# Inputs laid out by the launch: x turned, the columns of w_ada over the partitions, weights as blocks

## The chip, the core and the metric

The kernel runs on one core of a Trainium2 chip. The metric is device time in microseconds (us); the time before is the median of three runs, 811.69 us (811.64 to 811.93). An execution has been profiled with the hardware profiler, and all rows below come from it. Names: PE is TensorE (matrix products), PEld its weight loads, DVE is VectorE, ACT is ScalarE, POOL is GpSimd, SP is SyncE, which issues most of the DMAs. The laying out of the inputs, which the change adds, is done by the host ahead of the launch and is not in the measured time.

## What is computed

One decoder layer for 256 tokens of width 2048 with float32 weights: a conditioned norm, one wide projection, two attention mixers, two branch projections and an output projection.

```python
ada = c @ w_ada + b_ada                       # c: (1, 2048), w_ada: (2048, 6144)
shift, scale, gate = jnp.split(ada, 3, axis=-1)
h = rms_norm(x, g_pre) * (1.0 + scale[:, None, :]) + shift[:, None, :]
proj = h @ w_in                               # (256, 2048) @ (2048, 11824)
...                                           # sparse attention (A), dilated windows (B)
merged = jax.nn.sigmoid(ma) * ya + jax.nn.sigmoid(mb) * yb
out = merged @ w_out
return x + (gate[:, None, :] * rms_norm(out, g_post))
```

## The kernel before

**Split products.** A product takes h, or its like, as a high and a low part (xH, xL), and each weight tile as a high part (wH, rounded by ACT, L539) and a low part (wL, the remainder by DVE, L540). Three matmuls add up: wH with xH (L609), wH with xL (L611), wL with xH (L614); lines L599 to L604 are the same with the sides exchanged. Only the first pass, over the first 128 of the 2048 features, multiplies unsplit f32 (L585, L589).

**The stream of items.** All weights come as a list of items of up to 128 x 1024 floats, in a fixed order: `w` items are weight tiles, `ada` items are pieces of w_ada for shift and scale, `gate` items are the rest of w_ada, `ck` items belong to attention A. SP loads them (`dma`, L512 to L521) into seven buffers named raw; when an item's buffer is free again the seventh item after it is issued. Three items ahead of the product, `prep` splits a weight (L539, L540) or adds an `ada` item to a sum (L556, L558: sum += raw times one value of c per partition). `main` issues the products and `evac` empties the PSUM banks.

**Features in passes.** h is not known at once, since scale and shift need 16 MB of w_ada. So features come in groups (feature blocks of 128: 0; 1 to 2; 3 to 6; 7 to 9; 10 to 12; 13 to 15). For each group the `ada` items run ahead of the weight items that need it. When its last item is in, `make_h` (L273) turns the sums on PE (L282: the 128 partial sums of a column lie over the partitions, so a transpose brings them into a row), adds them on DVE (L283), adds the bias and forms h from xT, the normed and turned x.

**The start.** x arrives in two megabytes with tokens on partitions. ACT and DVE each square half (L170, L172, with a sum along the row), DVE forms 1/rms (L180 to L192). c, b_ada and g_pre arrive as rows and are turned on PE (L143). For feature block 0 the sums over w_ada are PE products (L241) and a DVE share (L257, L259). `keep_warm` issues products whose result nobody reads. The first h ends with L299 (tile hF), and L589 is the first product of the stream.

**The side work.** `side_main` is a list of steps, of which one is issued beside each item: x of each later group is normed on POOL (L223) and turned on PE (L230), then the tables of angles, masks, and the two attentions. Position weights pe_ck and pe_cv are turned there, too (L808). Within each engine the order is what the tile scheduler makes of this program; `behind` adds an order without a wait.

Of the kernel before, what the change touches and what calls it, by code (L numbers as in the profile page):

```python
# [44 lines left out]
def hybrid_block(tc, x, c, positions, w_ada, b_ada, g_pre, g_post, w_in, pe_ck, pe_cv, w_ck1, w_ck2,  # L45
                 w_cv1, w_cv2, w_br_a, w_br_b, w_out, out):
    with ExitStack() as ctx:
        _build(ctx, tc, x, c, positions, w_ada, b_ada, g_pre, g_post, w_in, pe_ck, pe_cv, w_ck1, w_ck2,
               w_cv1, w_cv2, w_br_a, w_br_b, w_out, out)


def _build(ctx, tc, x, c, positions, w_ada, b_ada, g_pre, g_post, w_in, pe_ck, pe_cv, w_ck1, w_ck2,
           w_cv1, w_cv2, w_br_a, w_br_b, w_out, out):
# [36 lines left out]
    vc = work.tile([16, 128], F32, name="vc", tag="PT", bufs=2)  # L90
    vec = work.tile([48, 128], F32, name="vec", tag="PT", bufs=2)
    xs = big.tile([128, NT, D], F32, name="xs", tag="ma")
    for t in range(NT):
        DMA.dma_start(xs[:, t, :], x[0, t * 128:(t + 1) * 128, :])
    A.dma_start(vc, c[0].rearrange("(a p) -> a p", p=128))
    A.dma_start(vec[0:32, :], b_ada[0, 0:2 * D].rearrange("(a p) -> a p", p=128))
    A.dma_start(vec[32:48, :], g_pre[0].rearrange("(a p) -> a p", p=128))
# [27 lines left out]
    cT, bT, gT = vecT[:, 0:16], vecT[:, 16:48].rearrange("p (h k) -> p h k", h=2), vecT[:, 48:64]
# [26 lines left out]


    n0 = (PASSES[0][1] - PASSES[0][0]) * 128
    nb0 = n0 // 128
    ST = big.tile([128, 4, 1024], F32, name="ST", tag="mb")
    acc0 = ST[:, 1, 0:2 * n0].rearrange("p (h n) -> p h n", h=2)
    raws0 = []
    for q in range(4):
        r = wp.tile([128, 4, 2, n0], F32, name="raw0", tag="raw", bufs=RAW)  # L160
        for half in range(2):
            DMA.dma_start(r[:, :, half], rows(w_ada[0], 4 * q, 4, half * D, n0))
        raws0.append(r)


    ssq = const.tile([128, NT], F32)
    ssp = const.tile([128, NT, 2], F32)
    for t in range(NT):
        lo, hi = slice(0, D // 2), slice(D // 2, D)
        i_sq = A.activation(ST[:, 2], xs[:, t, lo], AF.Square, accum_out=ssp[:, t, 0:1])  # L170
        with behind(i_id, i_c):
# [1144 lines left out]
```

## Time and profile before

| What | Value |
|---|---|
| Median of three runs | 811.69 us |
| Span of the profiled execution, first to last instruction | 808.8 us |
| PE busy | 790.9 us, 98% |
| DVE busy | 673.6 us, 83% |
| ACT busy | 443.2 us, 55% |
| POOL busy | 90.1 us, 11% |
| Read from memory | 190.38 MB |
| First product of the stream (L589) | 18.18 us after the span's start |

The page gives a single time for the profiled execution, its span. A record of a matmul lasts until its result has drained, so records overlap, and a busy PE isn't PE at its peak; the distance from one record's start to the next says what a matmul costs in a stream. A chain of waits follows the end back: at each step to what released it. A table by stage cuts the span into stretches.

### The profile page before, as it was taken

The numbers are of one execution on the slowest core, as the hardware profiler recorded it, in microseconds if no ns is written. First come the engines' busy times: TensorE is split into PE (matmuls) and PEld (weight loads), VectorE is DVE, ScalarE is ACT, GpSimd is POOL, SyncE is SP. The second block draws the span as 40 slices with busy tenths as digits, with TensorE's granted clock in tenths as the row PEclk, the third lists the DMA queues.
The fourth block names the chain that finished last, engine by engine and source line by source line (L and its number), as shares of the span: only waits on it lengthen the run. The fifth ranks groups of instructions, "written<-read, shape, count | busy, mean of one in ns | idle before, by whom it ended". The sixth has DMA issues, their size and how long they took to land.

```text
span 808.8 us, 11963 instructions
## 1 busy us (share of the span) xinstructions
PE 790.9 (98%) x4181; PEld 665.5 (82%) x4181; DVE 673.6 (83%) x1033; ACT 443.2 (55%) x731; POOL 90.1 (11%) x111
## 2 busy tenths in 40 slices
PE   7999999999999999999999999999999999999995
PEld 4588988899887889788889999888888888888884
DVE  6799899999996979898878997778796888867464
ACT  2767564443444655587776777555644344444451
POOL 4300000000000027064312121001100000000000
PEclk9999999999999999999999999999999999999998
DMA  9999989999896578644344435557789989976523
GB/s 334 361 371 294 321 295 321 344 309 341 268 365 218 168 223 260 192 143 144 118 145 122 140 111 168 180 178 237 227 267 296 304 287 327 316 246 222 190 102 104
DMA packets 106951, 193.25 MB, mean 239 GB/s; under 512 B 7594, under 2 KB 36618, under 8 KB 106252
## 3 DMA queue, kind: packets, MB, share of 16 engines
q1 hardware_dynamic: 105344, 189.16, 71.2%
q10 hardware_dynamic: 1548, 3.34, 1.2%
q8 instruction: 33, 0.54, 0.3%
q14 instruction: 26, 0.21, 0.1%
HBM read 190.38 MB, written 2.10 MB: 238 GB/s over the span
## 4 chain that ended last, share of the span: by engine, by line
PE 90%; DVE 5%; DMA 2%; issue 1%; ACT 1%; POOL 0%; DVEq 0%; SPq 0%; POOLq 0%; ACTq 0%
PE mm L609 23%; PE mm L611 23%; PE mm L614 22%; PE mm L599 3%; PE mm L604 3%; PE mm L601 3%; PE mm L589 2%; PE pt_ps L999 1%; PE sA L963 1%; DVE wL L540 1%; DMA xs<-in_x_dram 1%; PE mm L585 1%; DVE ST L558 1%; DMA raw<-in_w_in_dram 1%; PE pvb_ps L1140 1%
## 5 line engine op out<-in xcount | busy, mean ns | idle before, releaser
L539 ACT ACTIVATE wH<-raw 128x1024 fp32r<-128x1024 f32 (+2 forms) x268 | 267.9, 1000 | 276.3 <-PE mm L611 204.4
L540 DVE TENSOR_TENSOR wL<-raw,wH 128x1024 fp32r<-128x1024 f32 (+2 forms) x268 | 315.6, 1181 | 90.6 <-ACT wH L539 85.6
L609 PE MATMUL mm<-wH,xH 128*128 128x512 f32 (+2 forms) x616 | 237.3, 387 | 0.0
L611 PE MATMUL mm<-wH,xL 128*128 128x512 f32 (+2 forms) x616 | 234.4, 382 | 0.0
L614 PE MATMUL mm<-wL,xH 128*128 128x512 f32 (+2 forms) x616 | 189.9, 383 | 0.0
L611 PEld LDWEIGHTS mm<-wH,xL 128*128 128x128 f32 x616 | 115.9, 188 | 20.1
L609 PEld LDWEIGHTS mm<-wH,xH 128*128 128x128 f32 x616 | 115.8, 188 | 20.0 <-ACT mm L629 0.3
L614 PEld LDWEIGHTS mm<-wL,xH 128*128 128x128 f32 x616 | 113.6, 188 | 22.0 <-DVE wL L540 0.3
L558 DVE SCALAR_TENSOR_TENSOR ST<-raw,vecT,ST 128x768 f32<-128x768 f32 (+2 forms) x75 | 76.5, 1020 | 1.8 <-DMA raw<-in_w_ada_dram 1.5
L599 PE MATMUL mm<-xH,wH 128*128 128x256 f32 x240 | 62.5, 281 | 0.0
L601 PE MATMUL mm<-xL,wH 128*128 128x256 f32 x240 | 62.0, 279 | 0.0
L609 PE MATMUL mm<-wH,yH 128*128 128x512 f32 x128 | 50.4, 394 | 0.0
L609 PE MATMUL mm<-wH,mH 128*128 128x512 f32 x128 | 50.0, 391 | 0.0
L611 PE MATMUL mm<-wH,yL 128*128 128x512 f32 x128 | 49.9, 389 | 0.0
L611 PE MATMUL mm<-wH,mL 128*128 128x512 f32 x128 | 49.8, 389 | 0.0
L604 PE MATMUL mm<-xH,wL 128*128 128x256 f32 x240 | 49.2, 279 | 0.0
L599 PEld LDWEIGHTS mm<-xH,wH 128*128 128x128 f32 x240 | 45.0, 188 | 0.1
L601 PEld LDWEIGHTS mm<-xL,wH 128*128 128x128 f32 x240 | 45.0, 188 | 0.1
L558 DVE SCALAR_TENSOR_TENSOR gacc<-raw,vecT,gacc 128x1024 f32<-128x1024 f32 x32 | 41.0, 1283 | 0.0
L614 PE MATMUL mm<-wL,mH 128*128 128x512 f32 x128 | 39.8, 389 | 0.0
L614 PE MATMUL mm<-wL,yH 128*128 128x512 f32 x128 | 39.4, 389 | 0.0
L604 PEld LDWEIGHTS mm<-xH,wL 128*128 128x128 f32 x240 | 37.3, 188 | 0.0
(306 smaller groups left out, 1016.3 us busy)
## 6 DMA issues: line engine op xcount, KB each, us to landing
raw<-in_w_in_dram SPq DMA_DIRECT2D x165, 512.0 KB, 4.6
raw<-in_w_ada_dram SPq DMA_DIRECT2D x48, 512.0 KB, 5.0
raw<-in_w_ada_dram SPq DMA_DIRECT2D x48, 384.0 KB, 4.9
raw<-in_w_out_dram SPq DMA_DIRECT2D x32, 512.0 KB, 4.8
raw<-in_w_br_a_dram SPq DMA_DIRECT2D x16, 512.0 KB, 6.4
raw<-in_w_br_b_dram SPq DMA_DIRECT2D x16, 512.0 KB, 5.8
raw<-in_w_in_dram SPq DMA_DIRECT2D x29, 256.0 KB, 3.5
raw<-in_w_ada_dram SPq DMA_DIRECT2D x24, 256.0 KB, 5.6
```

The costliest lines, as they stand in the source:

```text
L539: highest[0] = A.activation(H, raw, AF.Copy)
L540: lowest[0] = V.tensor_tensor(L, raw, H.bitcast(F32), op=OP.subtract)
L558: V.scalar_tensor_tensor(acc, r, cc, acc, op0=OP.mult, op1=OP.add)
L585: T.matmul(job.ps[t][:, b * S:(b + 1) * S], lhsT=it.raw[:, j, c0:c0 + 128], rhs=hj, start=(first and j == 0 and b == 0), stop=(last and j ...
L589: i_mm = T.matmul(job.ps[t][:, :job.n], lhsT=hj[:, t * 128:(t + 1) * 128], rhs=it.raw[:, j, cs], start=(first and j == 0), stop=(last and ...
L599: T.matmul(ps, lhsT=it.H[:, j, bs], rhs=sH[:, it.kt0 + j, :], start=(first and j == 0 and b == 0), stop=False, skip_group_check=True)
L601: T.matmul(ps, lhsT=it.H[:, j, bs], rhs=sL[:, it.kt0 + j, :], start=False, stop=False, skip_group_check=True)
L604: T.matmul(ps, lhsT=it.L[:, j, bs], rhs=sH[:, it.kt0 + j, :], start=False, stop=(last and j == it.nk - 1), skip_group_check=True)
L609: T.matmul(ps, lhsT=sH[:, it.kt0 + j, ts], rhs=it.H[:, j, cs], start=(first and j == 0), stop=False, skip_group_check=t in job.seeded)
L611: T.matmul(ps, lhsT=sL[:, it.kt0 + j, ts], rhs=it.H[:, j, cs], start=False, stop=False, skip_group_check=t in job.seeded)
L614: T.matmul(ps, lhsT=sH[:, it.kt0 + j, ts], rhs=it.L[:, j, cs], start=False, stop=(last and j == it.nk - 1), skip_group_check=t in job.seeded)
L963: T.matmul(o, lhsT=QT[:, u.t, h // 2, h % 2, :], rhs=KTt[:, hl, :, 0:128] if u.t == 0 else KTt[:, hl, u.br, :], start=(hl == 0), stop=(hl ...
```

## The change

The host lays the inputs out anew: x turned (feature on the partition), c, b_ada, g_pre and the position weights already as columns in one array of 128 x 96, positions as one array, and for shift and scale the array w_ss, in which a partition holds one column of w_ada, so 2048 values in a row. All weight items lie one behind the other in the order in which the kernel loads them, each as a block in which a partition's values are one contiguous piece (4 KB for 1024 floats).

In the kernel, c is spread over all partitions once (four f32 products with a row of ones, L142, copied to cB). An `ada` item is then 128 columns by 1024 rows, and DVE multiplies it with cB and sums along the row in one instruction (L529), of which a feature block needs four: 60 in all beyond block 0, where there were 80 instructions over 72 items. The turns of sums and their reductions (L282, L283) go. x is squared without a sum and summed over the partitions with one-column products (L186); 1/rms is spread by two products (L225), POOL multiplies the turned x with it (L751), and the turns of x (L230) go. Weight items, products, passes and attention stay as they are.

```diff
-    for t in range(NT):
-        DMA.dma_start(xs[:, t, :], x[0, t * 128:(t + 1) * 128, :])
...
+    A.dma_start(crow, d_in["c"])
+    for q in range(4):
+        DMA.dma_start(xs[:, 4 * q:4 * q + 4, :], d_in["xT"][:, 4 * q:4 * q + 4, :])
+    A.dma_start(small, d_in["small"])
+    A.dma_start(pos_i, d_in["pos"])
...
+            i_c = T.matmul(ps, lhsT=ones[0:1, :], rhs=crow[:, j * 512:(j + 1) * 512], start=True, stop=True)
...
+    def c_halves():
+        for j in (1, 3):
+            last = A.activation(cB[:, j // 2, 512:1024], c_ps[j], AF.Copy)
+        return last
...
+        if q < 3:
+            with behind(*last_sq):
+                last_sq = [A.activation(sq, xq, AF.Square)]
+            G.tensor_tensor(sq[:, 0:512], sq[:, 0:512], sq[:, 512:1024], op=OP.add)
+            if q == 0:
+                with behind(*last_sq):
+                    last_sq = [c_halves()]
...
+                    i_ss = T.matmul(ss_ps[:, t, 0:1], lhsT=sq[:, k * S + t * 128:k * S + (t + 1) * 128],
+                                    rhs=ones[:, 0:1], start=(q == 0 and k == 0 and t == 0),
...
+    def sum0(q, half, after):
+        r = raws0[q][:, half]
+        with behind(after):
+            return V.scalar_tensor_tensor(r, r, 1.0, cB[:, q // 2, q % 2 * 512:(q % 2 + 1) * 512], op0=OP.mult,
+                                          op1=OP.mult, accum_out=sums0[:, half, q:q + 1])
...
-                for i in range(m):
-                    for j in range(n):
-                        T.transpose(ps[:, i, j, :], acc[:, half + i, j * 128:(j + 1) * 128], ident)
-                V.tensor_reduce(AB[:, half:half + m, a:b], ps, axis=AX.X, op=OP.add)
...
+    def weights(name, kt0, nk, c0, n):
+        at = placed[0]
+        plan.append((name, kt0, nk, c0, n))
+        placed[0] += 128 * nk * n
+        w = d_in["weights"]
+        return bass.AP(tensor=w.tensor, offset=w.offset + at, ap=[[nk * n, 128], [1, nk * n]])
...
+            if it.kind == "ada":
+                r = raw[:, 0, :]
+                V.scalar_tensor_tensor(r, r, 1.0, cB[:, it.q], op0=OP.mult, op1=OP.mult,
+                                       accum_out=sums[:, it.half, it.kt0, it.q:it.q + 1])
...
-            for t in range(NT):
-                with behind(*first_h):
-                    x_norm(G, a, b, t)
-                    x_turn(a, b, t)
-                yield
+            G.tensor_tensor(xT[a], xs[:, a:b, :], rstdB[:, None, :].to_broadcast([128, b - a, S]), op=OP.mult)
+            yield
```

**Order on PE around the first products.** Before, from the turn of b_ada and g_pre to the second pass (ada_ps: sums for block 0, x_ps: turns of x for block 0, xT_ps: turns of later x):

```order
L143 MATMUL v_ps<-ident,vec 128x48
L241 MATMUL ada_ps<-vecT,raw_136 128x128 x8
L251 MATMUL x_ps<-ident,xs 128x128 x2
L241 MATMUL ada_ps<-vecT,raw_142 128x128 x6
L264 MATMUL ada_ps<-ones_r,ST 128x128 x2
L589 MATMUL mm<-raw,hF 128x512 x8
L230 MATMUL xT_ps<-ident,xs 128x128 x2
L589 MATMUL mm<-raw,hF 128x256 x2
L230 MATMUL xT_ps<-ident,xs 128x128 x4
L282 MATMUL ada_ps<-ident,ST 128x128 x4
```

Now, with six, eight and six warm-ups (L135) behind the first, the second and the third row (c_ps: c spread, ss_ps: sums of squares, rB_ps: 1/rms spread):

```order
L142 MATMUL c_ps<-ST,ones_r 128x512 x4
L186 MATMUL ss_ps<-ones_r,sqs 128x1 x20
L225 MATMUL rB_ps<-ident,rstd 128x128 x2
L564 MATMUL mm<-raw,hF 128x512 x8
L564 MATMUL mm<-raw,hF 128x256 x2
L564 MATMUL mm<-raw,hF 128x304 x2
L564 MATMUL mm<-raw,hF 128x512 x12
L560 MATMUL mm<-hF,raw 128x256 x16
L582 MATMUL mm<-wH,xH 128x512
```

Nothing stands between the products of the first pass any more, and ahead of them the sums of w_ada have left PE.

**Order on ACT at the start.** Before (xs: x, v_ps: turned rows, rtx: the root):

```order
L170 ACTIVATE ST,ssp<-xs 128x1024 x2
L145 ACTIVATE vecT<-v_ps 128x48
L186 ACTIVATE rtx<-ssq 128x2
L268 ACTIVATE ST<-x_ps 128x256
L301 ACTIVATE xH<-hF 128x256
```

Now (sqs: squares, ST<-c_ps: the two copies of spread c):

```order
L172 ACTIVATE sqs<-xs 128x1024
L153 ACTIVATE ST<-c_ps 128x512 x2
L172 ACTIVATE sqs<-xs 128x1024 x2
L179 ACTIVATE sqs<-xs 128x512
L212 ACTIVATE rtx<-ssq 128x2
L232 ACTIVATE rstdB<-rB_ps 128x256
L284 ACTIVATE xH<-hF 128x256
```

The second and third square now stand behind the copies of c, which wait for PE.

**Order on DVE at the start, now** (raw_139 to raw_148: block 0 of w_ss, sums_184: its row sums). Before, the two squares with their sums and the five multiplications of block 0 stood here:

```order
L148 COPY ST<-c_ps 128x512 x2
L181 TENSOR_TENSOR sqs<-xs 128x512
L194 SCALAR_TENSOR_TENSOR raw_139,sums_184<-raw_139,ST 128x512 x2
L194 SCALAR_TENSOR_TENSOR raw_142,sums_184<-raw_142,ST 128x512 x2
L205 TENSOR_SCALAR ssq<-ss_ps 128x2
L194 SCALAR_TENSOR_TENSOR raw_145,sums_184<-raw_145,ST 128x512
L218 SCALAR_TENSOR_TENSOR rstd<-tfx,rtx 128x2
L194 SCALAR_TENSOR_TENSOR raw_148,sums_184<-raw_148,ST 128x512 x2
L260 SCALAR_TENSOR_TENSOR ST<-xs,small,rB_ps 128x256
L275 TENSOR_REDUCE AB<-sums_184 128x2
L283 TENSOR_SCALAR hF<-ST,AB 128x256
```

Four of the eight row sums of block 0 stand behind the mean square, three of them behind the root.

More of the change, by code (lines that the diff above doesn't have):

```diff
@@ L155, in _build @@
-    nb0 = n0 // 128
-    ST = big.tile([128, 4, 1024], F32, name="ST", tag="mb")
-    acc0 = ST[:, 1, 0:2 * n0].rearrange("p (h n) -> p h n", h=2)
+    with behind(keep_warm(8)):
+        c_ps = []
+        for j in range(4):
+            ps, _ = product_bank("c_ps")
+            i_c = T.matmul(ps, lhsT=ones[0:1, :], rhs=crow[:, j * 512:(j + 1) * 512], start=True, stop=True)
+            c_ps.append(ps)
+    with behind(i_c):
+        i_warm = keep_warm(6)
+    with behind(i_mask):
+        for j in (0, 2):
+            i_cV = V.tensor_copy(cB[:, j // 2, 0:512], c_ps[j])
@@ new lines, in _build @@
+    sums0 = const.tile([128, 2, 5], F32)
+    def sum0(q, half, after):
[3 more added lines that the diff above has]
+                                          op1=OP.mult, accum_out=sums0[:, half, q:q + 1])
+    with behind(i_sq):
+        V.tensor_copy(sums0[:, 0, 4:5], bT[:, 0, 0:1])
+        i_sum = V.tensor_scalar(sums0[:, 1, 4:5], bT[:, 1, 0:1], 1.0, None, op0=OP.add)
@@ L182, in rsqrt @@
+    for q in range(2):
+        for half in range(2):
+            i_sum = sum0(q, half, i_sum)
+    ssq = const.tile([128, NT], F32)
+    with behind(i_sum):
+        i_ssq = V.tensor_scalar(ssq, ss_ps[:, :, 0], 1.0 / D, EPS, op0=OP.mult, op1=OP.add)
+    i_sum = sum0(2, 0, i_ssq)
     def rsqrt(dst, ms, name):
@@ L191, in rsqrt @@
                                    op0=OP.mult, op1=OP.mult)
-        V.scalar_tensor_tensor(dst, tf, 1.5, rt, op0=OP.add, op1=OP.mult)
-        return ih
+        return V.scalar_tensor_tensor(dst, tf, 1.5, rt, op0=OP.add, op1=OP.mult)
     rstd = const.tile([128, NT], F32)
-    rsqrt(rstd, ssq, "x")
+    with behind(i_sum):
+        i_sum = rsqrt(rstd, ssq, "x")
+    rB_ps = psum.tile([128, S], F32, name="rB_ps", tag="pv")
+    for t in range(NT):
+        i_rB = T.matmul(rB_ps[:, t * 128:(t + 1) * 128], lhsT=rstd[:, t:t + 1].to_broadcast([128, 128]), rhs=ident,
+                        start=True, stop=True)
+    with behind(i_ss):
+        keep_warm(8)
+    with behind(i_rB):
+        keep_warm(6)
+    rstdB = const.tile([128, S], F32)
+    A.activation(rstdB, rB_ps, AF.Copy)
     xH = big.tile([128, KT, S], F32R, name="xH")
@@ L245, in _build @@
-    with behind(turn):
-        ada0_part(0)
-    x0_ps = psum.tile([128, nb0, S], F32, name="x0_ps", tag="pt")
-    for t in range(NT):
-        i_x = x_norm(V, 0, nb0, t)
-        for j in range(nb0):
-            T.transpose(x0_ps[:, j, t * 128:(t + 1) * 128], xs[:, t, j * 128:(j + 1) * 128], ident)
-    on_dve = 5
-    for kt in range(4, 4 + on_dve):
-        r, cc = raws0[kt // 4][:, kt % 4], cT[:, kt:kt + 1]
-        if kt == 4:
-            with behind(i_x):
-                V.tensor_scalar(acc0, r, cc, None, op0=OP.mult)
-        else:
-            V.scalar_tensor_tensor(acc0, r, cc, acc0, op0=OP.mult, op1=OP.add)
@@ L426, in w_item @@
         it.n = sum(j.n for j in jobs)
-        it.src = rows(w, kt0, nk, c0, it.n)
+        it.src = weights(w, kt0, nk, c0, it.n)
         return it
```

284 lines of the change are left out of this document (116 added, 168 removed).

## The prediction

> **What bounds the kernel now.** I read the page's busy table first, then a table by stage (columns: the stretch in us, then length and busy time with instruction counts of PE, PEld, DVE, ACT and POOL, then granted clock, share of the DMA engines, GB/s), then the chain of waits.
>
> ```profile
> PE 790.9 (98%) x4181; PEld 665.5 (82%) x4181; DVE 673.6 (83%) x1033; ACT 443.2 (55%) x731; POOL 90.1 (11%) x111
> ```
> ```profile
> 0.00:18.20 18.20, 13.33 (x75) 8.40 (x75) 12.52 (x38) 4.51 (x10) 7.47 (x14) 1.00 0.94 327
> 18.20:60.00 41.80, 41.80 (x169) 28.24 (x170) 35.52 (x88) 28.95 (x54) 8.84 (x7) 1.00 1.03 367
> 60.00:200.00 140.00, 140.00 (x792) 122.72 (x790) 133.94 (x164) 73.04 (x92) 0.00 (x0) 1.00 0.94 319
> 200.00:243.00 43.00, 43.00 (x195) 35.39 (x193) 41.15 (x48) 19.18 (x20) 0.00 (x0) 1.00 0.92 313
> 300.00:480.00 180.00, 176.00 (x1141) 155.56 (x1140) 160.74 (x307) 125.26 (x294) 57.06 (x71) 1.00 0.51 155
> 480.00:800.00 320.00, 320.00 (x1555) 268.51 (x1554) 239.80 (x311) 160.66 (x220) 10.41 (x9) 1.00 0.70 227
> ```
> ```profile
> PE 90%; DVE 5%; DMA 2%; issue 1%; ACT 1%; POOL 0%; DVEq 0%; SPq 0%; POOLq 0%; ACTq 0%
> ```
>
> From 18.2 us to 800 TensorE stops only in attention (4.0 us idle of 180). So there are three parts: a start in which PE produces nothing, a long stretch in which PE work is time, and a tail that the change leaves alone. Work taken from PE in the middle is worth its full spacing; work taken from DVE, ACT or the DMA queues there is worth nothing unless PE waits for it. DVE runs at 96% from 60 to 243 us and so must not get more work.
>
> **The change part by part.** *The start.* Rows of the timeline (start, length, engine, line, operation, tile, count, idle before and its releaser):
>
> ```profile
> 1.85 3.32 PE L137 MATMUL warm<-identb 128*128 128x512 bf16 x8 [1.85 <-DVE identb L80]
> 5.27 3.20 PE L137 MATMUL warm<-identb 128*128 128x512 bf16 x14
> 6.04 1.06 ACT L170 ACTIVATE ST<-xs 128x1024 f32<-128x1024 f32 x1 [2.42 <-DMA xs<-in_x_dram]
> 8.70 1.23 DVE L172 SCALAR_TENSOR_TENSOR ST<-xs 128x1024 f32<-128x1024 f32 x1 [1.16 <-DMA xs<-in_x_dram]
> 9.86 0.08 DVE L172 DVE_READ_ACCUMULATOR ST<-xs 128x1 f32 x1
> 10.62 0.16 DVE L180 TENSOR_SCALAR ssq<-ssq 128x2 f32<-128x2 f32 x1
> 11.63 0.16 DVE L192 SCALAR_TENSOR_TENSOR rstd<-tfx,rtx 128x2 f32<-128x2 f32 x1
> 12.76 2.40 PE L241 MATMUL ada_ps<-vecT,raw 128*128 128x128 f32 x20
> 17.44 0.69 DVE L299 TENSOR_SCALAR hF<-ST,AB 128x256 f32<-128x256 f32 x1
> 18.18 7.13 PE L589 MATMUL mm<-raw,hF 128*128 128x512 f32 x16 [1.24 <-DVE hF L299]
> 19.35 0.60 ACT L702 ACTIVATE CV<-mm 128x512 f32<-128x512 f32 x1 [0.77 <-PE mm L589]
> 18.61 0.43 DVE L303 TENSOR_TENSOR xL<-hF,xH 128x256 fp32r<-128x256 f32 x1 [0.48 <-ACT xH L301]
> ```
> ```profile
> L994 POOL TENSOR_TENSOR P<-P,cf 128x512 f32<-128x512 f32 x24 | 27.5, 1144 | 83.7 <-DVE cf L992 59.4 <-PE mm L614 10.8 <-ACT mm L629 7.8
> ```
>
> Before, the first product starts at 18.18. For the new start I add these durations along the new order. x's two megabytes landed at 6.04 and 8.70, so the four half-megabyte pieces land near 4.7, 6.0, 7.4 and 8.7. PE is through with eight warm-ups at 5.1. The four products that spread c over the partitions are f32 with 512 columns; such a product is two records of the L589 row, 7.13/16 = 0.45 us each, less its drain 0.43, so 0.87: four end at about 8.75. ACT's order is square 0 (4.7 to 5.8), two copies of c, squares 1 and 2, half a square. The second copy needs c's fourth product: 8.75 + 0.60 = 9.35. Squares 1 and 2 then end at 10.4 and 11.5 although x was there at 6.0 and 7.4; the half ends at 12.1. POOL's additions (512 elements, 1.14) end at 11.6 and 12.7. PE's sums of squares come in this order: four for piece 1 after 11.6, four for piece 2 after 12.7, eight for piece 3. Each is an f32 product, two records; L241 gives 2.40/20 = 0.12 a record, so 0.24: 13.7, then 15.6. From there all is on DVE. Mean square 0.16; a row sum of 512, from 1.23 for 1024 with the read of 0.08, is about 0.69; from L180's end (10.78) to L192's end (11.79) the root takes 1.0; three more row sums 2.07; x0 0.43; the small sum 0.16; hF 0.35 to 0.69. 15.7 + 0.16 + 0.69 + 1.0 + 2.07 + 0.43 + 0.16 + 0.5 = 20.7. **First product at 20.7, +2.5 us.** Low end: if one-column products cost next to nothing and squares never wait, the last weights set it. At x's pace (1 MB in 2.66) the 2 MB of raw0 land at 14.0, then 0.69 + 0.43 + 0.16 + 0.5 gives 15.8, -2.4. High end: POOL's additions and the additions' readers late by 1 us, clock lost (below): +4.5.
>
> *PE work removed.* Thirty transposes of x (L230), thirty of the sums (L282), two of the position weights (L808), in groups of two to four:
>
> ```profile
> L230 PE MATMUL xT_ps<-ident,xs 128*128 128x128 f32 x30 | 4.9, 272 | 0.0
> L282 PE MATMUL ada_ps<-ident,ST 128*128 128x128 f32 x30 | 4.8, 274 | 0.5 <-DVE AB L283 0.5
> 38.22 0.60 PE L282 MATMUL ada_ps<-ident,ST 128*128 128x128 f32 x4
> 38.66 3.62 PE L585 MATMUL mm<-hF,raw 128*128 128x256 f32 x16
> 46.01 0.49 PE L230 MATMUL xT_ps<-ident,xs 128*128 128x128 f32 x3
> 46.26 0.48 PE L609 MATMUL mm<-wH,xH 128*128 128x512 f32 x1
> 242.85 0.40 PE L611 MATMUL mm<-wH,xL 128*128 128x512 f32 x1
> 243.73 0.55 PE L282 MATMUL ada_ps<-ident,ST 128*128 128x128 f32 x3 [0.49 <-DVE AB L283]
> ```
>
> The means are lengths; records overlap. What counts is the distance to the next product: four in 38.66 - 38.22 = 0.44 (0.11 each), three in 46.26 - 46.01 = 0.25 (0.083 each). 24 stand in groups of two and four: 2.6 us; 36 in threes: 3.0. The two L808 are allowed 0.2 each. **-6.0 us**, between -5.0 (every transpose at 0.083, L808 nothing) and -6.6. The stage table shows no PE idle where they stood, so nothing else fills the place. *One stall.* At 242.85 the next product would follow after 0.23; PE waits until 243.73 for L283, which no longer exists: **-0.65**, between 0 and -0.9.
>
> *Shift and scale on DVE.* Here lies the cover that has to hold.
>
> ```profile
> L558 DVE SCALAR_TENSOR_TENSOR ST<-raw,vecT,ST 128x512 f32<-128x512 f32 x15 | 11.8, 789 | 1.2 <-DMA raw<-in_w_ada_dram 1.0
> L558 DVE SCALAR_TENSOR_TENSOR ST<-raw,vecT,ST 128x768 f32<-128x768 f32 x45 | 45.5, 1012 | 0.4 <-DMA raw<-in_w_ada_dram 0.2
> L558 DVE SCALAR_TENSOR_TENSOR ST<-raw,vecT,ST 128x1024 f32<-128x1024 f32 x15 | 19.1, 1275 | 0.3 <-DMA raw<-in_w_ada_dram 0.3
> L172 DVE SCALAR_TENSOR_TENSOR ST<-xs 128x1024 f32<-128x1024 f32 x2 | 2.5, 1226 | 1.6 <-DMA xs<-in_x_dram 1.6
> L283 DVE TENSOR_REDUCE AB<-ada_ps 128x3 f32<-128x384 f32 x6 | 3.3, 550 | 0.0
> L283 DVE TENSOR_REDUCE AB<-ada_ps 128x4 f32<-128x512 f32 x3 | 2.1, 689 | 2.4 <-PE ada_ps L282 2.4
> ```
>
> The rows before cost 11.8 + 45.5 + 19.1 = 76.4 us and 5.4 for the reductions. Sixty row sums have the form of L172, 1.226: 73.6. DVE gets 8.2 us lighter by 243 us and had 6.3 + 6.1 + 1.9 = 14.2 idle: hidden, 0. *DMA layout.* The bytes of every item stay, the pieces grow to a whole row of a partition; PE waits for no landing after 18.2 us: 0. SP is left with 32 issues fewer, none is moved past another. *xT on POOL*: 3840 elements at 1.144/512 are 8.6 us, done by 27, and PE first needs them near 38: 0. Ten ACT copies go from an engine at 55%: 0. *Attention.* Fewer side steps shift which product stands beside which score; its 4.0 us of idle may move either way: 0, within 2 us.
>
> Sum: 2.5 - 6.0 - 0.65 = -4.15. The page gives the profiled execution by its span, 808.8; the median of the runs, 811.69, lies 2.9 above it, taken as what surrounds the span and kept. 808.8 - 4.15 + 2.9 = **807.5 us**.
>
> **The rivals.** *The start is not late* (0.24). The squares' chain ends before DVE is through with its row sums. For it: one-column products may be far cheaper than 0.24. Against it: squares 1 and 2 stand behind c's fourth product whatever these cost. First product at 15.8 to 18.2: 802.6 to 805.
>
> *A cold start* (0.12). PE does only one-column products and waits from 10 to 15.6. The first eight warm-ups took 3.32 us, fourteen later ones 3.20, that is 0.42 and 0.23 each. Eight products' worth at the slow pace cost 3.32 - 8 x 0.23 = 1.5 more: 809.0. Against it: the fourteen warm-ups around the root. [...]
>
> *The transposes' time comes back as waits* (0.08). With PE earlier by 3 us, wL arrives late between 60 and 243 us, where DVE has 8 us of idle; the gain of 6.65 is lost and the start remains: 811.7 to 814.
>
> *Row sums at half speed* (0.04; slower). If a multiply of two f32 tiles with a sum took twice L172's 1.226, sixty would add 73.6 us; 14.2 + 8.2 of room leaves 51 on the path: about 859. It decides from (22.4 + 4.15)/60 = 0.44 us more, 1.67 a sum. [...] The trace speaks against it: L172 is that form, though both its sources are one tile, and is no slower than L558's 1.275.
>
> **How the numbers follow.** Forecast 0.50, then 0.24, 0.12, 0.08, 0.04, and 0.02 for a mishap in attention. 0.2% is 1.6 us, about what a measurement of this kernel can tell from none. Faster (under 810.1): 0.50 + 0.24 + 0.10 = 0.84. Same: 0.02 + 0.08 = 0.10. Slower: 0.06. The range reaches from the early start, 802.8, to the edge of the third rival, 811.0.
>
> **What would show it.** The first L564 record at 19.5 to 22 with ACT idle before square 1; L529 near 1.23 us; no PE idle from there to 300 us; PE's busy time some 6 us less. Wrong if PE waits for wL before 243 us, or if L564 begins before 18.

## The result: slower, not faster

The changed kernel took 817.44 us (median of four executions, 814.65 to 819.82) against 811.66 for the kernel before on the same chip: a ratio of 1.0069, 95% interval 1.0044 to 1.0094. Forecast were 807.5 us and a range up to 811.0. One thing has to be known to read its times: the unaltered kernel has two starts, which differ by 5 us, and an execution has the one or the other (eight of eleven took 814.2 to 816.0, three 818.9 to 819.8). The profile below is of the shorter one, 814.65 us with a span of 812.9, which is 4.1 more than the 808.8 before.

The busy table of the changed kernel, and its table by stage in the stretches of the prediction (stretch, length, busy time and count of PE, PEld, DVE, ACT, POOL, granted clock, DMA share, GB/s):

```profile
PE 795.0 (98%) x4125; PEld 663.7 (82%) x4125; DVE 671.2 (83%) x1074; ACT 441.3 (54%) x722; POOL 90.8 (11%) x109
```
```profile
0.00:18.20 18.20, 16.02 (x63) 9.57 (x64) 11.63 (x31) 6.15 (x8) 5.81 (x12) 0.85 0.89 330
18.20:60.00 41.80, 38.71 (x119) 22.22 (x118) 33.70 (x93) 24.60 (x45) 11.24 (x6) 0.90 0.79 278
60.00:200.00 140.00, 139.25 (x780) 121.52 (x779) 134.11 (x199) 72.87 (x91) 0.00 (x0) 1.00 0.92 333
...
243.00:300.00 57.00, 57.00 (x263) 47.11 (x262) 45.16 (x68) 31.08 (x41) 6.35 (x11) 1.00 0.60 202
300.00:480.00 180.00, 176.59 (x1130) 155.19 (x1129) 156.19 (x301) 123.29 (x287) 55.76 (x70) 1.00 0.49 157
```

All of the loss lies ahead of 80 us. From 18.2 to 60 us, where PE had no idle time before, it now idles 3.1 us, the clock reads 0.90, and the loads move 278 GB/s instead of 367. From 200 to 300 us all is as forecast, PE has no idle time there; the half microsecond that it waited at 243 is gone.

**The start.** Rows of the timeline of the changed kernel (start, length, engine, line), then the table by stage in narrow stretches:

```profile
5.38 3.86 PE L142 MATMUL c_ps<-ST,ones_r 1*128 1x512 f32 x8
9.17 2.74 PE L135 MATMUL warm<-identb 128*128 128x512 bf16 x6
11.70 2.26 PE L186 MATMUL ss_ps<-ones_r,sqs 128*128 128x1 f32 x16
14.29 3.75 PE L186 MATMUL ss_ps<-ones_r,sqs 128*128 128x1 f32 x24 [0.32 <-POOL sqs L173]
17.90 3.15 PE L135 MATMUL warm<-identb 128*128 128x512 bf16 x7
20.84 1.06 PE L225 MATMUL rB_ps<-ident,rstd 128*128 128x128 f32 x4
23.87 12.48 PE L564 MATMUL mm<-raw,hF 128*128 128x512 f32 x32
...
9.77 1.99 ACT L172 ACTIVATE sqs<-xs 128x1024 f32<-128x1024 f32 x2
...
10.90 3.33 POOL L173 TENSOR_TENSOR sqs<-sqs 128x512 f32<-128x512 f32 x2 [3.61 <-ACT sqs L172]
...
10.73 0.69 DVE L194 SCALAR_TENSOR_TENSOR raw<-raw,ST 128x512 f32<-128x512 f32 x1
11.57 1.53 DVE L194 SCALAR_TENSOR_TENSOR raw<-raw,ST 128x512 f32<-128x512 f32 x1
13.04 1.74 DVE L194 SCALAR_TENSOR_TENSOR raw<-raw,ST 128x512 f32<-128x512 f32 x1
```
```profile
9.20:10.50 1.30, 1.30 (x5) 0.47 (x5) 1.23 (x4) 1.23 (x2) 0.00 (x0) 0.50 0.97 312
18.00:20.80 2.80, 2.80 (x8) 1.10 (x7) 2.65 (x13) 0.20 (x1) 0.00 (x0) 0.50 0.66 259
```

The first product comes at 23.87, not at 20.7. Up to ACT's squares all is within 0.6 us of the forecast. Then three things differ. PE runs at half clock from 9.2 to 12.6 and again from 16.0 to 22.8 (it reads 0.50): six warm-ups take 2.74 us, so the sums of squares begin at 11.7, and their later records are 0.21 us apart instead of 0.11. POOL's additions take 1.67 us each instead of the 1.14 of the forecast (the first one, which met no row sum, took 1.26), and DVE's row sums beside them 1.53 and 1.74 instead of 0.69: they hold each other up. And the spreading of 1/rms (L225) stands behind warm-ups of 0.43 us, so that it starts 1.2 us after 1/rms is there.

**Pass 0.** Rows of the timeline, what SP's queue waits for DVE's row sums in the whole execution (us in total, times, longest), and a row of the table by stage:

```profile
22.40 11.09 POOL L751 TENSOR_TENSOR xT<-xs,rstdB 128x512 f32<-128x512 f32 x5 [8.17 <-ACT rstdB L232]
24.30 2.01 DVE L286 TENSOR_TENSOR xL<-hF,xH 128x256 fp32r<-128x256 f32 x1 [0.48 <-ACT xH L284]
26.23 2.83 DVE L529 SCALAR_TENSOR_TENSOR raw<-raw,ST 128x1024 f32<-128x1024 f32 x1
29.09 0.33 SPq L501 DMA_DIRECT2D raw<-in_weights_dram  x1
31.75 2.82 DVE L529 SCALAR_TENSOR_TENSOR raw<-raw,ST 128x1024 f32<-128x1024 f32 x1
34.50 1.21 DVE L529 SCALAR_TENSOR_TENSOR raw<-raw,ST 128x1024 f32<-128x1024 f32 x1
37.17 3.67 PE L564 MATMUL mm<-raw,hF 128*128 128x512 f32 x8 [0.82 <-DMA raw<-in_weights_dram]
43.11 5.37 PE L564 MATMUL mm<-raw,hF 128*128 128x512 f32 x8 [2.27 <-DMA raw<-in_weights_dram]
```
```profile
SPq L501 <- DVE raw L529: 66.1, 56, 7.2
```
```profile
24.00:30.00 6.00, 6.00 (x15) 2.65 (x16) 5.70 (x4) 3.97 (x9) 6.00 (x3) 1.00 0.19 68
```

While POOL multiplies the later x by 1/rms (22.4 to 33.5), three row sums take 2.8 us each; the next, with POOL done, takes 1.21. A row sum reads a raw buffer, and SP loads the next item only into a free one. So SP, whose last issue ended at 21.8, issues nothing until 29.09 (its longest wait for a row sum is 7.2 us), the loads fall to 68 GB/s between 24 and 30 us, and PE runs out of weights twice: 0.82 + 2.27 us. After the second wait the clock is down (it reads 0.50 from 43.3 to 46.7 us), and the same eight records take 5.37 us instead of 3.67.

**The account.** The distances between the starts of PE's records, beyond what is usual for their shape, add up to 5.3 us from the first product to 60 us (0.4 before) and 1.65 from 60 to 80 (0.28 before). From 300 to 480 us PE idles 0.6 us less than before. With the start: 5.7 + 4.9 + 1.4 - 0.6 - 6.65 (the forecast gain in the middle) = +4.75, and measured is +4.1. The terms are good to some half a microsecond. So the gain was there, and three losses ate it.

### The profile page after: what moved, and what is told of

It reads as the page before. It is cut to its first block, busy times and chain, and to the rows that moved or that the text cites. A ratio compares the mean times of both kernels' runs of the same rounds, so it can differ in the third digit from the quotient of the medians.

```text
span 812.9 us, 11775 instructions
## 1 busy us (share of the span) xinstructions
PE 795.0 (98%) x4125; PEld 663.7 (82%) x4125; DVE 671.2 (83%) x1074; ACT 441.3 (54%) x722; POOL 90.8 (11%) x109
## 4 chain that ended last, share of the span: by engine, by line
PE 93%; DVE 3%; issue 1%; ACT 1%; DMA 1%; POOL 0%; DVEq 0%; ACTq 0%
PE mm L582 23%; PE mm L587 23%; PE mm L584 23%; PE mm L577 3%; PE mm L572 3%; PE mm L574 3%; PE mm L564 2%; PE pt_ps L959 1%; PE sA L923 1%; PE warm L135 1%; PE mm L560 1%; DMA raw<-in_weights_dram 1%; DVE wL L521 1%; PE pvb_ps L1100 1%; PE sB L1090 1%
## 5 line engine op out<-in xcount | busy, mean ns | idle before, releaser
L529 DVE SCALAR_TENSOR_TENSOR raw<-raw,ST 128x1024 f32<-128x1024 f32 x60 | 77.4, 1299 | 3.6 <-DMA raw<-in_w_ss_dram 3.6
L533 DVE SCALAR_TENSOR_TENSOR gacc<-raw,small,gacc 128x1024 f32<-128x1024 f32 x32 | 40.9, 1278 | 0.0
L954 POOL TENSOR_TENSOR P<-P,cf 128x512 f32<-128x512 f32 x24 | 27.1, 1128 | 94.6 <-DVE cf L952 51.7
```

Of the source, the lines that this page charges most:

```text
L529: V.scalar_tensor_tensor(r, r, 1.0, cB[:, it.q], op0=OP.mult, op1=OP.mult, accum_out=sums[:, it.half, it.kt0, it.q:it.q + 1])
L533: V.scalar_tensor_tensor(acc, raw[:, 0, :], cT[:, it.kt0:it.kt0 + 1], acc, op0=OP.mult, op1=OP.add)
L954: G.tensor_tensor(pv, pv, cf[:, :u.nb, None].to_broadcast([128, u.nb, u.len]), op=OP.mult)
```

## The experiments

The theory after the result had two parts. **Shared access**: POOL and DVE, each reading f32 tiles, hold each other up; that slows the row sums, frees the raw buffers late and starves PE. **Cold start**: the new start feeds PE with products of one row (L142) or one column (L186), which do not keep the clock up. The rivals were that the new **layout** lands more slowly, that DVE carries **too much** work, and that the gain of 6.65 in the middle never existed.

### The changed kernel again, and without POOL's multiplication

> The changed kernel once more, unaltered, as the base of this group (its four executions so far took 814.65 to 819.82 us, the kernel before 811.1 to 811.93). If the spread is a property of the kernel, times again scatter over some 5 us (814 to 820) and before stays within 1 us; if it was one chip's, they agree within 1 us. Theory of the buffers and theory of the layout both expect the rows of the first profile again: the first three row sums L529 near 2.8 us, no loads between 26 and 30 us, PE waiting for weights near 36 and 41 us.

Measured: 814.76 us, seven executions from 814.15 to 819.61; ratio 1.0050 (1.0032 to 1.0068), and the kernel before stayed within 810.3 to 812.9 in sixteen, wider than the 1 us expected. Both starts occur again, so the spread belongs to the kernel. The profiled one is of the longer start, 819.61:

```profile
5.38 7.19 PE L142 MATMUL c_ps<-ST,ones_r 1*128 1x512 f32 x8
15.04 8.53 PE L186 MATMUL ss_ps<-ones_r,sqs 128*128 128x1 f32 x40
29.40 2.84 PE L564 MATMUL mm<-raw,hF 128*128 128x512 f32 x6 [0.41 <-DVE hF L283]
```
```profile
18.00:24.00 6.00, 6.00 (x29) 5.69 (x29) 0.39 (x2) 0.20 (x1) 0.00 (x0) 1.00 0.29 112
```

All of PE's records up to 26 us are twice as far apart as at full clock, c's 0.85 us instead of 0.43 (from start to start; 0.90 is their length of 7.19 over eight), the sums of squares 0.21 throughout, and the first product comes 5.5 us later; the span grows by 4.9. So the lateness of the start passes through nearly whole. The clock column reads 1.00 up to 24 us all the same, over records twice as far apart, where in the shorter start it read 0.50 over such records (16.0 to 18.0 us): in these executions it showed a clock that had risen and fallen, and not one that had yet to rise.

```diff
-            G.tensor_tensor(xT[a], xs[:, a:b, :], rstdB[:, None, :].to_broadcast([128, b - a, S]), op=OP.mult)
+            with behind(*first_h): A.activation(xT[a], xs[:, a:b, :], AF.Copy)
```

> The multiplication of the later x by 1/rms (L751, POOL) is replaced by a plain copy on ACT, so 1/rms is left out of all feature blocks but the first: POOL does nothing between 22 and 39 us. Theory of the buffers (POOL's multiplication slows DVE's row sums, the raw buffers come free late, the loads stop and PE runs dry): L529 is 1.2 to 1.25 us from the first on and L286 0.45, the pause in the loads at 26 to 30 us shrinks to under 1.5 us, PE's waits at 36 and 41 us (0.82 + 2.27 us, and 1.7 us of products at half clock behind them) go: 4 to 5 us less than the unaltered kernel of this group, some 812 against 817. Theory of the layout (blocks of 4 KB rows land more slowly): L529 is short, the waits stay, at most 1 us less.

Measured: four executions from 808.81 to 809.09 and six from 814.26 to 815.43, so 5.7 and 5.0 us less than the unaltered kernel with the same start. The table by stage (36 to 60 us), and the row sums up to 60 us (line, count, busy us, mean ns):

```profile
36.00:60.00 24.00, 24.00 (x95) 17.67 (x94) 19.48 (x34) 17.44 (x29) 0.00 (x0) 1.00 0.96 358
```
```profile
L529 DVE SCALAR_TENSOR_TENSOR raw<-raw,ST 128x1024 f32<-128x1024 f32 x13 | 15.6, 1220 | 4.3 <-DMA raw<-in_w_ss_dram 4.3
```

Every row sum is at 1.22, PE has no idle time and the clock stays up. That bears out the shared access, and it is more than the 4 to 5 us expected. The loss from 60 to 80 us stays as it was (PE idles 0.82 us there, 0.75 in the changed kernel), so it has another cause.

### The layout undone

```diff
-        return bass.AP(tensor=w.tensor, offset=w.offset + at, ap=[[nk * n, 128], [1, nk * n]])
+        return d_in[name][kt0 * 128:(kt0 + nk) * 128, c0:c0 + n].rearrange("(a p) n -> p a n", p=128)
```

> The weight items are loaded from the untouched arrays again, in rows of 1 to 2 KB as before the change; all else is the changed kernel. Prediction's step (layout: 0) and theory of the buffers: the same time as the unaltered kernel of this group within 1 us, the pause at 26 to 30 us stays. Theory of the layout: the waits of PE at 36 and 41 us shrink, 3 us less or better.

Measured: 819.52 us (817.17 to 821.13), 4.8 more than the unaltered kernel, but with another share of the two starts. Three of the four executions, 819.39 to 821.13, lie by the longer start of the unaltered kernel (818.88 to 819.82); the fourth, 817.17, lies between its two starts. The profiled execution, 819.39, has the longer start, as has the one of the unaltered kernel above, 819.61, and the two are alike. PE's wait for weights between 24 and 60 us, with the untouched arrays, and then with the blocks:

```profile
PE mm L561 <- DMA raw<-in_w_in_dram: 2.6, 1, 2.6
```
```profile
PE mm L564 <- DMA raw<-in_weights_dram: 2.6, 2, 1.8
```

The wait is the same 2.6 us. The rival needed 3 us less with the layout undone, and no execution shows that: it falls, and the step on the DMA layout, 0, stands to within some 1.5 us. Why the longer start came three times in four is not known.

### The start: which shapes keep the clock

```diff
-            i_c = T.matmul(ps, lhsT=ones[0:1, :], rhs=crow[:, j * 512:(j + 1) * 512], start=True, stop=True)
+            for i in range(4): i_c = T.matmul(ps[:, i * 128:(i + 1) * 128], lhsT=cT[:, 4 * j + i:4 * j + i + 1].to_broadcast([128, 128]), rhs=ident, start=True, stop=True)
```

> c is spread over the partitions by sixteen 128-row products with the unit matrix (c as columns from the array of small vectors, whose load goes first) instead of four products with a single row. Theory of the cold start (products with one row leave the clock to fall: it reads 0.50 from 9.2 to 12.5 us): the clock reads 1.00 there, the six warm-ups behind take 0.22 us each instead of 0.43, the one-column products begin near 10.5 instead of 11.7; the first product of the stream comes 0.5 to 1.5 us earlier than 23.87. If the start's lateness goes through to the end, the time falls by as much; if the pause of the loads decides, by less than 0.5 us. If the clock falls for another reason (waits), it reads 0.50 as before.

Measured: 815.86 us (813.96 to 816.18). The timeline:

```profile
9.75 1.46 PE L135 MATMUL warm<-identb 128*128 128x512 bf16 x6
14.62 5.28 PE L186 MATMUL ss_ps<-ones_r,sqs 128*128 128x1 f32 x24 [0.60 <-POOL sqs L173]
```

Half right. The six warm-ups behind c take 1.46 us instead of 2.74, and none of four executions had the longer start. But the clock then falls during the one-column products (it reads 0.98 from 9 to 14 us and 0.50 from 14 to 24), 24 of them take 5.28 us, and the first product, at 25.79, is later than before the edit, not earlier.

```diff
-    with behind(keep_warm(8)):
+    with behind(keep_warm(16)):
         c_ps = []
```

> Sixteen warm-ups ahead of the products that spread c instead of eight. The unaltered kernel has two starts: in one the products of c take 0.43 us a record and the first product of the stream comes at 23.87, in the other 0.90 a record and it comes at 29.40, and the times fall into 814 to 816 and 819 to 820. Theory of the missed window (eight warm-ups, 3.4 us, sometimes don't fill the window after which the clock rises, and the one-row products behind them don't count as work): with sixteen the second start never occurs, all executions within 1.5 us; the warm-ups 9 to 16 at 0.22 each put c's products to begin near 7.1 instead of 5.38, so the median is 814.5 to 816.5. If the two starts have another cause, executions at 819 to 822 still occur.

Measured: 816.91, 817.47 and 819.67 us; a fourth execution took 2820.43, which nothing here explains and which is left out. The profiled one (819.67):

```profile
7.73 4.99 PE L142 MATMUL c_ps<-ST,ones_r 1*128 1x512 f32 x8
15.18 8.53 PE L186 MATMUL ss_ps<-ones_r,sqs 128*128 128x1 f32 x40
```

A miss: a start as long still occurs (first product at 29.35), although the clock had risen at 6.58 us, before c's products began (twelve warm-ups take 4.26 us, where in the unaltered kernel four at the slow pace took 1.91). It falls at 9.99, in the midst of them (the table by stage reads 0.60 from 9 to 14 us), and reads 0.50 from 14 to 24 over the one-column products. So here it did not suffice that the clock had risen; what stood behind the warm-ups mattered, too.

What decides between the two starts of the unaltered kernel can be read from the traces in part. In the shorter start the trace has the clock change at 5.75, 9.16, 12.57, 15.99 and 22.81 us, steps of 3.41 us or twice that, and the eight warm-ups (1.85 to 5.38) fill most of the 3.41 us ahead of 5.75. In two profiled executions of the longer start the clock first rises at 27.41 (the unaltered kernel; seven warm-ups from 27.23 take 1.77 us, which is nearly the full pace, 1.67) and at 26.73 (the layout undone; four records of L225 from 26.37 take 0.79 us, between 1.06 and 0.71). An estimate from these numbers: counted back in the same steps, each has one step that begins before the warm-ups and a next one that ends among c's products, so the warm-ups fill none. No run set where the steps lie, or showed steps ahead of the first rise: that this decides the start is argued, not shown.

```diff
-    ss_ps = psum.tile([128, NT, 2], F32, name="ss_ps", tag="pt")
+    ss_ps = psum.tile([128, NT, 128], F32, name="ss_ps", tag="pt")
...
-                    i_ss = T.matmul(ss_ps[:, t, 0:1], lhsT=sq[:, k * S + t * 128:k * S + (t + 1) * 128],
-                                    rhs=ones[:, 0:1], start=(q == 0 and k == 0 and t == 0),
+                    i_ss = T.matmul(ss_ps[:, t, :], lhsT=sq[:, k * S + t * 128:k * S + (t + 1) * 128],
+                                    rhs=ones, start=(q == 0 and k == 0 and t == 0),
```

With this and c spread as above:

> c spread by 128-row products, and the sums of squares by products with 128 columns of ones instead of one column (same values, same number of products); POOL's multiplication stays. Theory of the cold start: products with one row or one column leave the clock low, 128 by 128 products don't. Then records of the sums of squares stay at 0.11 us (not 0.21) to the end, the warm-ups behind take 0.22, the first product comes at 21 to 22, and the time falls with it by 2 to 2.5 us against the 814.8 of the unaltered kernel: 812 to 813, one start only. If the fall of the clock comes from gaps on PE and not from the shape, the records double again after 15 us and the time is 814 to 816 as with c alone.

Measured: 812.44 us, ten executions from 811.77 to 813.69, one start only. The timeline:

```profile
13.72 2.94 PE L186 MATMUL ss_ps<-ones_r,sqs 128*128 128x128 f32 x24 [0.52 <-POOL sqs L173]
```

As expected: the same 24 records, now 128 columns wide, take 2.94 us instead of 5.28, and the first product comes at 21.42. PE waits for POOL ahead of them nearly as long as with c alone (0.52 and 0.60 us), so the gap is not what makes the difference. 128 columns cost no more than one there (0.11 us from record to record), and over them the clock reads 1.00 (9 to 24 us).

### POOL's part given to DVE, and all together

```diff
-            G.tensor_tensor(xT[a], xs[:, a:b, :], rstdB[:, None, :].to_broadcast([128, b - a, S]), op=OP.mult)
+            with behind(*first_h): V.tensor_tensor(xT[a], xs[:, a:b, :], rstdB[:, None, :].to_broadcast([128, b - a, S]), op=OP.mult)
```

> The multiplication of the later x by 1/rms is done by DVE instead of POOL, so the result is whole; start unaltered. Theory of the shared access (two f32 operands of DVE and of POOL at once slow each other): row sums at 1.2 us, the five multiplications 0.7 to 1.25 each, 4.6 in all, no wait for landings at 36 to 46 us; two starts as before: 809 to 810.5 in one, 814.5 to 816 in the other, 4 to 5.5 less than the unaltered kernel in each. If DVE's 4.6 us more fall on the path, 2 to 3 us less only.

Measured: 809.65 and 812.19 us in two executions, 815.02 to 816.74 in eight. Against the unaltered kernel (814.8 in the middle with the shorter start, 819.6 with the longer) that is 5.1 and 2.6 us less in the two, and about 4 less in the eight: nearly what was expected. DVE has room for most of the 4.6 us.

```diff
-            G.tensor_tensor(sq[:, 0:512], sq[:, 0:512], sq[:, 512:1024], op=OP.add)
+            with behind(i_cV, i_mask): V.tensor_tensor(sq[:, 0:512], sq[:, 0:512], sq[:, 512:1024], op=OP.add)
...
-    for q in range(2):
+    for q in range(3):
         for half in range(2):
             i_sum = sum0(q, half, i_sum)
```

With these, and the edits to c, to the sums of squares and to xT (below: the combined kernel):

> All together: c by 128-row products, sums of squares by 128 columns, the three additions of squares and the multiplication of x on DVE, six of the eight row sums of block 0 ahead of the mean square. By the two theories: sums of squares end near 16, the first product comes at 19.5 to 20.5, row sums at 0.69 and 1.22 throughout, no pause of the loads over 2 us; against the 808.9 with the multiplication off POOL and the first product at 23.87, 3 to 4 us less: 804.5 to 806.5, about 6 us below the kernel before, one start only. If pass 0 is bound by the loads, the earlier start is lost there: 808 to 809.

Measured, as expected: 806.45 us (805.86 to 807.70), ratio to the kernel before 0.9942 (0.9927 to 0.9956), first product at 20.32.

### What is left, and what the removed work was worth

```diff
-                r = raw[:, 0, :]
-                V.scalar_tensor_tensor(r, r, 1.0, cB[:, it.q], op0=OP.mult, op1=OP.mult,
+                r = raw[:, 0, 0:512]
+                V.scalar_tensor_tensor(r, r, 1.0, cB[:, it.q, 0:512], op0=OP.mult, op1=OP.mult,
```

> The combined kernel with row sums L529 over 512 of the 1024 columns, so half of the sum over w_ada is left out of shift and scale beyond block 0: DVE gets 60 x 0.53 = 32 us less, most of it before 243 us. What remains in the combined kernel is PE waiting for wL (L521) between 59 and 80 us, 1.7 us in three places, with DVE busy all of 20 us there. If DVE's load is the cause, these waits go and the time falls by 1.5 to 2.5 us to 804 to 805; the prediction's step (row sums hidden: 0) would have it unchanged within 0.7 us.

Measured: 804.14 us (804.07 to 804.91), 2.3 less than the combined kernel, as the theory of DVE's load expected. The stretch from 60 to 80 us of the combined kernel, and with half the sums:

```profile
60.00:80.00 20.00, 18.78 (x83) 14.47 (x82) 20.00 (x32) 10.99 (x15) 0.00 (x0) 1.00 0.92 323
```
```profile
60.00:80.00 20.00, 19.60 (x99) 16.79 (x100) 19.43 (x33) 13.10 (x18) 0.00 (x0) 1.00 0.96 362
```

In the combined kernel DVE is busy without a gap there (20.00), and PE idles 1.22 us; with half the sums it idles 0.40. So in this one stretch the row sums were not hidden.

```diff
+            for t in range(NT):
+                pt = psum.tile([128, 4, 128], F32, name="xT_ps", tag="s", bufs=2)
+                with behind(*first_mm):
+                    for j in range(b - a):
+                        T.transpose(pt[:, j, :], xs[:, a + j, t * 128:(t + 1) * 128], ident)
...
+                        T.transpose(ps[:, i, j, :], xT[a][:, j, (half + i) * 128:(half + i + 1) * 128], ident)
```

> The combined kernel (806.45) with the sixty transposes back on PE at the places where they stood: thirty of x in pass 0 and thirty at the forming of h, in groups of two to four; nobody reads their results. The prediction's step (PE work removed: 6.0 for 62 transposes, its whole spacing, nothing fills the place) expects 5.6 us more (4.7 to 6.2): 811 to 812.7. If PE has slack in pass 0 or waits for wL anyway, so that removing them gained little, it is 0 to 3 us more: 806.5 to 809.5.

Measured: 813.42 us (811.80 to 815.66), 7.0 more than the combined kernel and above the 811 to 812.7 expected. The sixty transposes in PE's groups, and the stretch from 60 to 80 us:

```profile
L275 PE MATMUL ada_ps<-ident,xT 128*128 128x128 f32 x30 | 4.9, 278 | 0.0
L763 PE MATMUL xT_ps<-ident,xs 128*128 128x128 f32 x30 | 4.1, 273 | 0.0
```
```profile
60.00:80.00 20.00, 19.40 (x95) 16.09 (x95) 20.00 (x32) 11.71 (x15) 0.00 (x0) 1.00 0.90 296
```

From the start of one to the start of what follows they take 5.99 us in sum, 0.10 each. The gain forecast for their removal is real. Its size in the time is known less well: the executions scatter by 3.9 us, and the two profiled spans, 810.6 and 805.8, differ by 4.8 instead of 7.0. Part of that is the start: the first product comes at 19.51 here and at 20.32 in the combined kernel, though the edit doesn't touch the start. And from 60 to 80 us PE idles 0.60 us with the transposes and 1.22 without, so a small part of the removed work does come back as waits.

```diff
-    with behind(i_c):
-        i_warm = keep_warm(6)
+    i_warm = i_c
...
-            with behind(i_cV, i_mask): V.tensor_tensor(sq[:, 0:512], sq[:, 0:512], sq[:, 512:1024], op=OP.add)
+            with behind(i_mask): V.tensor_tensor(sq[:, 0:512], sq[:, 0:512], sq[:, 512:1024], op=OP.add)
...
-            if q == 0:
+            if q == 2:
                 with behind(*last_sq):
                     last_sq = [c_halves()]
```

> The combined kernel with a start in another order: ACT squares x before it copies c, DVE adds the squares as they come, and the six warm-ups between c and the sums of squares go. From the rows of the combined kernel: the sums of squares end near 14.3 instead of 16.4, 1/rms near 16, the first product of the stream comes at 18.4 instead of 20.3. If the start passes through to the end one for one, 804.3 to 805 (2 us less than the combined kernel); if pass 0 is now bound by the loads, less than 0.7 us less.

Measured: 803.98 us (803.85 to 804.58), ratio 0.9912 (0.9897 to 0.9927): 0.9% faster than the kernel before, and 0.3 us below the expected 804.3 to 805. The first product of the stream:

```profile
18.35 4.10 PE L564 MATMUL mm<-raw,hF 128*128 128x512 f32 x9
```

The first product comes 2 us earlier and the time falls by 2.5. This kernel starts 0.17 us later than the kernel before and has a span of 802.1, against 808.8: 6.7 less, and forecast was 6.65 for the middle. That the two agree so closely is in part luck, since this kernel has the multiplications on DVE and keeps some of the loss from 60 to 80 us.

> The fastest kernel so far (803.98; one start, first product at 18.35, as late as before the change) with one line as in the change: the multiplication of the later x by 1/rms on POOL instead of DVE. It prices the prediction's step (xT on POOL: 0) alone. Theory of the shared access: the first row sums take 2.8 us instead of 1.2, the raw buffers come free late, the loads pause and PE waits for weights: 4 to 6 us more, 808 to 810. If what cost time in the changed kernel was the late start together with POOL's multiplication, an early start leaves room for it: at most 1.5 us more. If DVE is glad to be rid of 4.6 us of multiplications: the same or less.

Measured, with that one line of the change put back into the fastest kernel: 810.26 us (809.60 to 810.93), 6.3 more, where the shared access expected 4 to 6 and the other two theories at most 1.5. Row sums from 16 to 60 us, and the table by stage:

```profile
L529 DVE SCALAR_TENSOR_TENSOR raw<-raw,ST 128x1024 f32<-128x1024 f32 x13 | 20.5, 1590 | 1.8 <-DMA raw<-in_w_ss_dram 1.8
```
```profile
24.00:36.00 12.00, 10.97 (x29) 4.91 (x27) 11.53 (x52) 7.70 (x15) 4.45 (x3) 1.00 0.79 259
36.00:60.00 24.00, 22.01 (x92) 17.05 (x93) 17.96 (x31) 15.58 (x26) 0.00 (x0) 1.00 0.97 358
```

With a warm and early start, where nothing else stands in the way, PE idles 1.03 us from 24 to 36 us and 1.99 from 36 to 60; with the multiplications on DVE it idles 0 and 0.42. By the distances between PE's records, 20 to 60 us loses 3.2 us more than without that line and 60 to 80 us 2.0 more; the first product comes 0.37 later, at 18.72. That is 5.6 of the 6.1 us between the two spans.

## Why the prediction was wrong, point by point

| Step of the prediction | Forecast, us | Measured, us | By |
|---|---|---|---|
| First product | +2.5, at most +4.5 | +5.7, or +11.2 in the other start | profiles of the two starts |
| xT on POOL | 0 | +4.9 by distances, +5.0 to +6.3 by times | profile; multiplication left out; put back alone |
| Row sums on DVE, hidden | 0 | +1.4, shared with the removed PE work | 60 to 80 us; half the sums; transposes put back |
| PE work removed | -6.0 | -5.99 by distances, -7.0 by times | sixty transposes put back |
| Stall at 243 us | -0.65 | gone | 57.00 of 57.00 us busy |
| DMA layout | 0 | 0, within 1.5 | layout undone |
| Attention | 0, within 2 | -0.6 | PE's idle time, 300 to 480 us |

**The step that failed first is xT on POOL: "3840 elements at 1.144/512 are 8.6 us, done by 27, and PE first needs them near 38: 0".** It asked when POOL's result is needed, and not what DVE does meanwhile. I had the row of POOL's speed from another stage, and took DVE's 1.226 as good beside it. In this place POOL works next to DVE for 11.1 us instead of 8.6, a row sum takes 2.8, and since a row sum holds a raw buffer, the late row sum is a late load, and the late load is an idle PE. The layout step's sentence, "PE waits for no landing after 18.2 us: 0", rested on buffers that come free in time. The profile before showed the loads at 367 GB/s there and a DMA share of 1.03, which left little room for a pause: from 24 to 36 us, loads at 291 GB/s cost PE nothing when the multiplication was left out, and loads at 155 in the changed kernel left it without weights soon after.

The last two instructions of POOL's multiplication show how the two get in each other's way:

```profile
27.94 2.79 POOL L751 TENSOR_TENSOR xT<-xs,rstdB 128x768 f32<-128x768 f32 x1
30.69 2.79 POOL L751 TENSOR_TENSOR xT<-xs,rstdB 128x768 f32<-128x768 f32 x1
```

They take turns. The row sum of 26.23 ends at 29.06, and POOL's instruction begun meanwhile ends 1.67 us later, at 30.73. The row sum of 28.99 ends 1.08 us after that, at 31.81, POOL's next 1.67 us after it, at 33.48, and the row sum of 31.75 1.09 us after that, at 34.57. So by these ends each waited until the other's instruction was through and then ran for about its own time: 1.22 us for a row sum alone, and 1.72 for POOL's 768 elements at L994's 1.144 for 512.

The row sums take 1.22 us alone (the kernel without the multiplication) and 2.83 beside POOL's multiplication, in turns with it. The prediction did not weigh such a price.

Yet the kernel before had POOL at work beside DVE, too, from 12 to 27 us: it normed x with an instruction that has one tensor operand (L223, TENSOR_SCALAR). DVE's multiplications with two tiles from 13 to 27 us, and then from 27 to 60, without POOL:

```profile
L558 DVE SCALAR_TENSOR_TENSOR ST<-raw,vecT,ST 128x512 f32<-128x512 f32 x8 | 6.6, 825 | 0.4 <-DMA raw<-in_w_ada_dram 0.3
```
```profile
L558 DVE SCALAR_TENSOR_TENSOR ST<-raw,vecT,ST 128x512 f32<-128x512 f32 x7 | 5.2, 747 | 0.8 <-DMA raw<-in_w_ada_dram 0.8
```

They lost a tenth, 0.83 us against 0.75, and the longest took 0.96, so they took no turns with POOL, whose instructions took 1.08 to 1.68 us each. So that POOL works beside DVE does not by itself tell the price. What differs is that POOL's new instruction reads two tensors, and that DVE's row sums write a sum; but xL (L286), which writes none, took 2.01 us beside the new instruction, too. So POOL's two tensors are the likelier reason; no run tests that alone.

The twofold time that the prediction weighed for a multiply of two f32 tiles with a sum is shown by no run: with its sources in different tiles a row sum alone takes 1.22 us.

**The start was mis-sized by more than its bounds.** The order of work was right and each engine's times were right as far as they were at full clock: c through at 9.2 (8.75 forecast), squares through at 11.8 (11.5). Wrong was the price of the PE work between: 0.24 for a one-column product, from L241, a product of 128 columns. At full clock it is no dearer, 0.22; but in the stream of it the clock fell (it reads 0.50 from 16.0 us on), and then it is 0.43. The rival "a cold start" had this cause and the right sign, but priced only eight products, 1.5 us, and counted on the fourteen warm-ups as its cure. Eight of them, at half clock, became a delay of their own. POOL's additions were costed from L994 as well, and met DVE's row sums as the multiplication did.

**"The transposes' time comes back as waits" was true in a small part**: 1.4 us from 60 to 80 us, not 6.65. "DVE runs at 96%" was a mean over 60 to 243 us. In its first part DVE had no gap even before the change. The table by stage of the kernel before, and its multiplications from 56 to 80 us; then the row sums of the changed kernel in the same stretch:

```profile
60.00:80.00 20.00, 20.00 (x101) 16.82 (x100) 20.00 (x27) 14.74 (x21) 0.00 (x0) 1.00 0.92 300
```
```profile
L558 DVE SCALAR_TENSOR_TENSOR ST<-raw,vecT,ST 128x1024 f32<-128x1024 f32 x6 | 7.6, 1273 | 0.0
```
```profile
L529 DVE SCALAR_TENSOR_TENSOR raw<-raw,ST 128x1024 f32<-128x1024 f32 x7 | 8.5, 1216 | 0.0
```

DVE was at 20.00 of 20.00 there, and seven row sums have taken the place of six multiplications: 0.9 us more on an engine without room. The relief of 8.2 us that the step counted on falls later. This is the same 1.4 us as in the table's row on the row sums: with half the sums or with the transposes back PE waits less there, and how the 1.4 divides between the two is not shown.

Right were the removed work, the stall, the layout, and that a late start passes through. What the transposes are worth in the time, between 4.8 and 7.0 us, stays open, and what decides between the two starts is argued only.

## What to carry to other kernels

Work moved to an idle engine was not free here: POOL's multiplication made DVE's row sums take 2.8 us instead of 1.2. So look at what the loaded engine does in the same microseconds, and at which buffer its instruction holds. On a stretch where the DMA engines have no idle time (their share was 1.03 from 18 to 60 us in the kernel before), price every long delay in the release of a buffer as a pause in the loads. And count a matmul by its shape, not by its being there: in the longer start products of one row and of one column kept PE busy for 15.7 us (7.19 and 8.53) with their records 0.85 and 0.21 us apart, twice the distance at full clock; with 128 columns a record took the 0.11 us that it takes with one at full clock, and the clock read 1.00.

## What the runs showed of the hardware

- PE's clock fell while PE was busy with thin products. With sixteen warm-ups PE was busy without a gap from 1.86 to 23.5 us; the clock rose at 6.58, fell at 9.99 among the one-row products and read 0.50 until 23.5 over the one-column ones, whose records lay 0.21 us apart instead of 0.11.
- In the longer start the granted clock read 1.00 up to 24 us while c's records lay 0.85 us apart and those of the sums of squares 0.21; with sixteen warm-ups, where the clock had risen before, it read 0.50 over records 0.21 us apart. The distances between records showed both.
- POOL's instructions with two tensors and DVE's slowed each other: two POOL additions took 3.33 us beside row sums, and 2.88 in an execution in which they met hardly one; row sums of 512 took 1.53 and 1.74 beside them and 0.69 alone. Even a DVE instruction with a single tensor operand (hF, L283) took 0.77 to 0.94 us beside POOL's multiplication and 0.41 without. POOL's instruction with one tensor operand, in the kernel before, cost DVE's multiplications a tenth (0.83 us against 0.75).
